# A hybrid RWKV-7 / latent-attention layer on one core: recurrence matmuls by head instead of by chunk parity, hi matmuls ahead of lo matmuls

## Chip, cores and metric

One core of a Trainium2 chip. The metric is device time in microseconds (us) of one execution of the kernel; lower is better.

## What is computed

One decoder layer, then a final norm, for 256 tokens of width 2048, all in float32. The parts that matter here:

```python
proj = rms_norm(x, attn_norm_g) @ w_in            # 35 column tiles of 128
# RWKV-7 group: 16 heads of 64; r, k, v, decay, a by token, then for each token t
state = state * w_t[:, None, :] + sa[..., None] * b_t[:, None, :] + v_t[..., None] * k_t[:, None, :]
y_t   = einsum('hvk,hk->hv', state, r_t)          # sa = state applied to a_t
y_rwkv = (group_norm(y) + bonus) * gate
# latent attention group: 8 heads, causal softmax
y = concat(y_rwkv, y_mla);  x = x + y @ w_out
x = x + conv_glu_ffn(rms_norm(x))                 # gate and up 2048 -> 5632, down 5632 -> 2048
```

## The kernel before, in words

**Dense products.** Every weight comes as pieces of 128x1024 float32 (512 KB) through SyncE's queue (`piece`, L121). ScalarE casts a piece to `hi` (L129), VectorE makes `lo = raw - hi` (L130), three buffers each. `prod_b` (L153) multiplies a piece of eight 128x128 weight blocks with activations that are themselves split in hi and lo: for each block j a matmul of `hi` with 512 moving columns (both parts of the activations, L157) and one of `lo` with 256 (L159), into one PSUM tile. It serves the input projection (`in_tile`), the up projections of the attention (`up_b`) and gate and up of the feed-forward part. `prod_a` (L169, L176 to L178) has the activations as weights and 512 moving columns throughout; it serves `wuv`, `wout` and the down projection.

**The recurrence.** The 256 tokens are cut into four chunks `c` of 64, c = 2w + par. `decay` (L391) makes the decays of two head pairs from two small matmuls (`lw` on array rows 0 to 63, `la` on rows 64 to 127). `gram` (L495) makes per head a 128x128 matrix of products within a chunk (`pg`, L507, 64 array rows each), masks it into `G1` on VectorE (L510), and sends blocks of it to a DRAM table `dL` (L519). `solve` (L540) reads `dL` back as `Lp` and inverts 32x32 triangles on VectorE (L548 to L554); `pR` and `pT` (L596, L609) join them into 64x64 inverses `TT`. `chunk(c)` (L624) then runs for both halves `hf` (8 heads each): `px` = state part (L635, one matmul of 128 moving columns for a pair of heads) plus local part (L639, 64x64); VectorE scales it into `xs` (L643); `TT` product (L648); ScalarE copies it into `UV` (L650); `pS` (L655) feeds the state update on VectorE (L674, L675); `py` = state part (L661) plus local part (L665), copied out by ScalarE (L678). The two heads of a pair are computed one after the other; the rows and columns of the array that a matmul uses depend on the parity of the chunk:

```python
rs_ = slice(par * 64, par * 64 + 64)
PE.matmul(px[rs_, a_ * P:(a_ + 1) * P], AR[pp][:, g, c, 0, :], ST[hf][:, a_, :], start=True, stop=True)
PE.matmul(px[rs_, e * 64:(e + 1) * 64], G1[c][hf][rs_, e, 0:64], UV[c][rs_, p, h * 64:h * 64 + 64], ...)
```

Each of these float32 matmul calls is two instructions in the trace (eight calls show as x16). The state update `pS` is the one product in which calls to the two column halves of the array (`hs`) already alternate.

**Order.** The program is written stage by stage; a scheduler of the framework puts each engine's instructions in order, and interleaves dense products of later stages (`mm`, on TensorE) with the recurrence. Engines run their lists in that order. `group_norm(w)` (L680) follows chunks 1 and 3; its VectorE work is interleaved too.

## Time and profile before

| | |
|---|---|
| time of the runs | 1240.6 us median of 3 (1240.4 to 1244.41) |
| the profiled execution: its own time, its span | 1240.28 us, 1238.5 us |
| busy: TensorE, VectorE, ScalarE, GpSimd | 97%, 67%, 48%, 5% |
| weights read | 210.48 MB, mean 174 GB/s of DMA |
| mean granted TensorE clock | 0.985 |

The busy time of a matmul in the trace includes its latency and overlaps the next one, so the pace of TensorE is read from the distance of one start to the next, not from the mean duration. Up to 75 us the kernel loads x and makes the first projections; Gram matrices come at 110 to 176 us, `solve` up to 244 us, the chunks from 255 to 361 us, softmax and attention up to 440 us, and from 490 us the feed-forward part.

### The profile page before, as it was taken

The page shows a single profiled execution, that of the slowest core. Times are in us where ns is not written, and L with a number is a line of the kernel's source. Part 1 is how long each engine was busy: PE and PEld are TensorE (multiplying, and loading weights), DVE is VectorE, ACT ScalarE, POOL GpSimd, SP SyncE. Part 2 cuts the span into 40 slices and gives each one's busy share as a digit, 9 for nine tenths or more (in the row PEclk, how much of TensorE's full clock was granted, in tenths as well). Part 3 has the DMA queues.
Part 4 walks back from the last instruction along what each step waited for, and adds up shares of the span by engine and source line. Part 5 has one row for each costly group of instructions (what it writes and reads, how often), then busy time and mean ns, then how long its engine had stood idle before and what let it go on. Part 6 is the DMA issues. An engine that isn't in the chain of part 4 may idle for free.

```text
span 1238.5 us, 18227 instructions
## 1 busy us (share of the span) xinstructions
PE 1206.4 (97%) x6897; PEld 1014.8 (82%) x6897; DVE 833.1 (67%) x1339; ACT 600.1 (48%) x931; POOL 56.6 (5%) x196
## 2 busy tenths in 40 slices
PE   6999979999999999999999999999999999999996
PEld 5778868888866788888888888888888888888885
DVE  6898749857766556777777776445567777775563
ACT  6784326534334445555555555333455555554452
POOL 4300000011011000100000000000000000000000
PEclk9999989999997999999999999999999999999999
DMA  8645444733423455555555555565655555566662
GB/s 298 212 133 158 132 124 140 217 120 112 133 69 102 153 171 181 167 194 190 187 188 187 187 188 187 187 202 190 199 190 187 187 188 187 187 220 211 213 204 88
DMA packets 70760, 215.80 MB, mean 174 GB/s; under 512 B 17360, under 2 KB 17616, under 8 KB 70672
## 3 DMA queue, kind: packets, MB, share of 16 engines
q1 hardware_dynamic: 69520, 211.84, 53.5%
q10 hardware_dynamic: 768, 2.05, 0.5%
q8 instruction: 54, 0.88, 0.3%
q0 software_dynamic: 384, 0.75, 0.2%
q14 instruction: 34, 0.28, 0.1%
HBM read 210.48 MB, written 3.41 MB: 173 GB/s over the span
## 4 chain that ended last, share of the span: by engine, by line
PE 93%; DVE 3%; DMA 2%; ACT 1%; issue 1%; POOL 1%; ACTq 0%; SPq 0%; DVEq 0%
PE mm L157 37%; PE mm L159 19%; PE mm L177 9%; PE mm L176 9%; PE mm L178 9%; PE pg L507 1%; PE px L639 1%; DVE lo L130 1%; PE px L648 1%; PE psc L819 1%; PE px L635 1%; PE py L665 1%; PE psc L817 1%; DMA raw<-in_win 1%; DMA cst<-in_cst 1%
## 5 line engine op out<-in xcount | busy, mean ns | idle before, releaser
L130 DVE TENSOR_TENSOR lo<-raw,hi 128x1024 fp32r<-128x1024 f32 x376 | 460.5, 1225 | 300.5 <-ACT hi L129 296.9
L129 ACT CAST hi<-raw 128x1024 fp32r<-128x1024 f32 x376 | 394.8, 1051 | 482.9 <-PE mm L157 232.0
L157 PE MATMUL mm<-z,hi 128*128 128x512 f32 x1408 | 493.5, 393 | 0.3 <-ACT hi L129 0.3
L159 PE MATMUL mm<-z,lo 128*128 128x256 f32 x1408 | 393.1, 279 | 0.8 <-DVE lo L130 0.8
L157 PEld LDWEIGHTS mm<-z,hi 128*128 128x128 f32 x1408 | 263.8, 187 | 63.4 <-ACT hi L129 0.6
L159 PEld LDWEIGHTS mm<-z,lo 128*128 128x128 f32 x1408 | 263.8, 187 | 1.2 <-DVE lo L130 1.1
L157 PE MATMUL mm<-x,hi 128*128 128x512 f32 x528 | 195.7, 408 | 16.7 <-DVE h L165 8.5
L159 PE MATMUL mm<-x,lo 128*128 128x256 f32 x528 | 153.8, 291 | 2.2 <-DVE lo L130 2.2
L157 PEld LDWEIGHTS mm<-x,hi 128*128 128x128 f32 x528 | 102.3, 194 | 41.0 <-ACT hi L129 8.2
L177 PE MATMUL mm<-lo,hh 128*128 128x512 f32 x336 | 130.7, 389 | 0.0
L178 PE MATMUL mm<-hi,hl 128*128 128x512 f32 x336 | 130.7, 389 | 0.0
L176 PE MATMUL mm<-hi,hh 128*128 128x512 f32 x336 | 119.4, 389 | 0.0
L159 PEld LDWEIGHTS mm<-x,lo 128*128 128x128 f32 x528 | 102.3, 194 | 5.4 <-DVE lo L130 2.7
L176 PEld LDWEIGHTS mm<-hi,hh 128*128 128x128 f32 x336 | 63.1, 188 | 13.2
L177 PEld LDWEIGHTS mm<-lo,hh 128*128 128x128 f32 x336 | 63.1, 188 | 13.1
L178 PEld LDWEIGHTS mm<-hi,hl 128*128 128x128 f32 x336 | 63.1, 188 | 13.0
L177 PE MATMUL mm<-lo,yhi 128*128 128x512 f32 x128 | 52.0, 406 | 0.1
L178 PE MATMUL mm<-hi,ylo 128*128 128x512 f32 x128 | 51.2, 400 | 0.0
L176 PE MATMUL mm<-hi,yhi 128*128 128x512 f32 x128 | 49.8, 403 | 0.0
L925 POOL MEMSET gt<- 128x2 f32 x44 | 4.4, 100 | 586.1 <-DVE hl L937 583.5
L177 PEld LDWEIGHTS mm<-lo,yhi 128*128 128x128 f32 x128 | 24.5, 192 | 6.2 <-DVE lo L130 0.5
L157 PE MATMUL mm<-cl,hi 128*128 128x512 f32 x80 | 29.6, 408 | 0.0
(284 smaller groups left out, 1189.7 us busy)
## 6 DMA issues: line engine op xcount, KB each, us to landing
raw<-in_wgu SPq DMA_DIRECT2D x176, 512.0 KB, 4.4
raw<-in_wdn SPq DMA_DIRECT2D x88, 512.0 KB, 4.3
raw<-in_win SPq DMA_DIRECT2D x70, 512.0 KB, 3.7
raw<-in_wout SPq DMA_DIRECT2D x32, 512.0 KB, 3.9
raw<-in_wuq SPq DMA_DIRECT2D x6, 512.0 KB, 3.8
xraw<-in_xT SPq DMA_DIRECT2D x4, 512.0 KB, 6.2
xt<-in_x SPq DMA_DIRECT2D x4, 512.0 KB, 6.7
raw<-in_wuk SPq DMA_DIRECT2D x4, 512.0 KB, 3.7
```

The lines of the kernel that those rows point to most:

```text
L129: S.copy(hi, raw)
L130: last_lo[0] = V.tensor_tensor(lo, raw, hi.bitcast(F32), ALU.subtract).ins
L157: PE.matmul(acc, hi[:, j * P:(j + 1) * P], ac, start=first and j == 0, stop=False, skip_group_check=True)
L159: PE.matmul(acc[:, :T], lo[:, j * P:(j + 1) * P], ac[:, 0, :], start=False, stop=last and j == n - 1, skip_group_check=True)
L176: PE.matmul(accs[tb], ah, wh, start=first and j == 0, stop=False)
L177: PE.matmul(accs[tb], ah, wl, start=False, stop=False)
L178: PE.matmul(accs[tb], al, wh, start=False, stop=last and j == n - 1)
L507: PE.matmul(pg[:, o:o + P], BK[pp][hs, gg, w, par * 2:par * 2 + 2, :], AR[pp][hs, gg, w * 2 + par, :, :], start=True, stop=True)
L635: PE.matmul(px[rs_, a_ * P:(a_ + 1) * P], AR[pp][:, g, c, 0, :], ST[hf][:, a_, :], start=True, stop=True)
L639: PE.matmul(px[rs_, e * 64:(e + 1) * 64], G1[c][hf][rs_, e, 0:64], UV[c][rs_, p, h * 64:h * 64 + 64], start=c == 0, stop=True, skip_group_ ...
L648: PE.matmul(pu[ru_, e * 64:(e + 1) * 64], TT[rs_, w * 16 + hf * 8 + e, :], xs[rs_, e * 64:(e + 1) * 64], start=True, stop=True, skip_group ...
L665: PE.matmul(py[rs_, e * 64:(e + 1) * 64], G1[c][hf][:, e, 64:128], UV[c][:, p, h * 64:h * 64 + 64], start=c == 0, stop=True, skip_group_ch ...
```

## The change

The rows of the recurrence are ordered by head of the pair: the first head of a pair always has output partitions 0 to 63 (array columns 0 to 63), the second 64 to 127, and calls of the two alternate (`pairs`). All contract over 128 rows: `XB`, a zeroed tile with the two heads' blocks on its diagonal, takes the place of `xs`; the lower half of `UV` starts at zero; the state part is two calls of 64 moving columns instead of one of 128. The chunk parity no longer picks rows. `xs` (one VectorE instruction per half) becomes two of `XB`, the copies to `UV` and `yt` become two each (one of the `UV` copies on VectorE), `dL` is written by 32 DMAs instead of 16, `pR` alternates its two column tiles, `gram` and `decay` issue the matmuls of the two row halves in turn, and `prod_b` issues the eight `hi` matmuls of a piece before its eight `lo` matmuls. Cut to its core:

```diff
--- before
+++ after
@@ prod_b
         hi, lo = pieces
         for j in range(n):
-            ac = act(kt0 + j)
-            PE.matmul(acc, hi[:, j * P:(j + 1) * P], ac, start=first and j == 0, stop=False,
+            PE.matmul(acc, hi[:, j * P:(j + 1) * P], act(kt0 + j), start=first and j == 0, stop=False,
                       skip_group_check=True)
-            PE.matmul(acc[:, :T], lo[:, j * P:(j + 1) * P], ac[:, 0, :], start=False,
+        for j in range(n):
+            PE.matmul(acc[:, :T], lo[:, j * P:(j + 1) * P], act(kt0 + j)[:, 0, :], start=False,
                       stop=last and j == n - 1, skip_group_check=True)
@@ decay
+        pw, pa = ch("lw"), ch("la")
         for g in range(2):
             p = pp * 2 + g
             cs = slice(g * T, (g + 1) * T)
-            pw, pa = ch("lw"), ch("la")
-            PE.matmul(pw[:, 0:T], lora[0:64, p * P:(p + 1) * P], wa[0:64], start=True, stop=True)
-            PE.matmul(pa[:, 0:T], lora[64:128, p * P:(p + 1) * P], wa[64:128], start=True, stop=True)
...
+            for rows, dst in ((slice(0, 64), pw), (slice(64, 128), pa)):
+                PE.matmul(dst[:, cs], lora[rows, p * P:(p + 1) * P], wa[rows], start=g == 0, stop=True,
+                          skip_group_check=True)
...
@@ gram
             for w in range(2):
+                pg = [ch("pg") for _ in range(2)]
+                for r in range(2):
+                    for gg in range(2):
+                        o = (r * 2 + gg) * P
+                        for h in range(2):
+                            hs = slice(h * 64, h * 64 + 64)
+                            PE.matmul(pg[h][:, o:o + P], BK[pp][hs, gg, w * 2 + r, :, :],
+                                      AR[pp][hs, gg, w * 2 + r, :, :], start=o == 0, stop=True,
+                                      skip_group_check=True)
                 for h in range(2):
-                    hs = slice(h * 64, h * 64 + 64)
-                    pg = ch("pg")
-                    for par in range(2):
-                        for gg in range(2):
-                            o = (par * 2 + gg) * P
-                            PE.matmul(pg[:, o:o + P], BK[pp][hs, gg, w, par * 2:par * 2 + 2, :],
-                                      AR[pp][hs, gg, w * 2 + par, :, :], start=True, stop=True)
...
                     for b in range(2):
-                        r0 = (1 - par) * 64 + b * 32
-                        k0 = par * 64 + b * 32 + w * 16 + hf * 8
-                        nc.sync.dma_start(dL[k0:k0 + 8].rearrange("e i t -> i e t"),
-                                          G1[c][hf][r0:r0 + 32, :, b * 32:(b + 1) * 32])
+                        r0 = 64 + b * 32
+                        for h in range(2):
+                            nc.sync.dma_start(dLv[b, c, :, h, hf * 4:hf * 4 + 4, :],
+                                              G1[c][hf][r0:r0 + 32, h * 4:h * 4 + 4, b * 32:(b + 1) * 32])
@@ UV
+    for c in range(4):
+        nc.gpsimd.memset(UV[c][64:128], 0.0)
...
-                S.copy(UV[w * 2 + par][rs_, pp * 2:pp * 2 + 2, :], ptv[rs_, :, w, :])
+                S.copy(UV[w * 2 + r][0:64, pp * 2:pp * 2 + 2, :], ptv[r * 64:r * 64 + 64, :, w, :])
@@ pR
-        for par in range(2):
-            r0, o0 = (1 - par) * 64, par * 64 + 32
-            for q in range(16):
-                qq = qh * 16 + q
-                PE.matmul(pr_[o0:o0 + 32, q * 32:(q + 1) * 32], G1[qh * 2 + par][q // 8][r0:r0 + 32, q % 8, 32:64],
-                          T11[0][r0:r0 + 32, qq, :], start=True, stop=True, tile_position=(r0, o0))
+        for q in range(16):
+            qq = qh * 16 + q
+            for h in range(2):
+                o0 = h * 64 + 32
+                PE.matmul(pr_[o0:o0 + 32, q * 32:(q + 1) * 32], G1[qq // 8][qq % 8 // 4][64:96, h * 4 + qq % 4, 32:64],
+                          T11[h][64:96, qq, :], start=True, stop=True, tile_position=(64, o0))
@@ chunk
+            def pairs(dst, terms):
+                for n, term in enumerate(terms):
+                    for a_ in range(4):
+                        p = hf * 4 + a_
+                        for h in range(2):
+                            lhsT, rhs = term(p, a_, h)
+                            PE.matmul(dst[HS[h], a_ * 64:(a_ + 1) * 64], lhsT, rhs,
+                                      start=n == 0 and a_ == 0, stop=True, skip_group_check=True)
+
+            def state(s):
+                return lambda p, a_, h: (AR[p // 2][:, p % 2, c, s, :], ST[hf][:, a_, HS[h]])
+
+            def local(s):
+                return lambda p, a_, h: (G1[c][hf][:, h * 4 + a_, s * 64:s * 64 + 64], UV[c][:, p, HS[h]])
+
+            pairs(px, ([state(0)] if c > 0 else []) + [local(0)])
+            for h in range(2):
+                V.tensor_tensor(XB[hf][HS[h], :, HS[h]], px[HS[h], 0:256].rearrange("p (a v) -> p a v", a=4),
+                                mtok[HS[h], c * 8 + hf * 4:c * 8 + hf * 4 + 4].unsqueeze(2).broadcast_to([64, 4, 64]),
+                                ALU.mult)
+            pu = px[:, 256:512]
+            pairs(pu, [lambda p, a_, h: (TT[:, c * 8 + p, :], XB[hf][:, a_, HS[h]])])
+            for h in range(2):
+                (S.copy if h else V.tensor_copy)(UV[c][64:128, hf * 4:hf * 4 + 4, HS[h]],
+                                                 pu[HS[h]].rearrange("p (a v) -> p a v", a=4))
             if c < 3:
                 pS = ch("pS")
...
+                pairs(pS, [lambda p, a_, h: (BKt[c][:, p, HS[h]], UV[c][:, p, HS[h]])])
+            pairs(py, ([state(1)] if c > 0 else []) + [local(1)])
...
-            ylast[c] = S.copy(yt[w][rs_, hf * 512:(hf + 1) * 512], py[rs_]).ins
+            for h in range(2):
+                yv = yt[w][rs_, hf * 512:(hf + 1) * 512].rearrange("p (a h v) -> p a h v", a=4, h=2)
+                ylast[c] = S.copy(yv[:, :, h, :], py[HS[h], 0:256].rearrange("p (a v) -> p a v", a=4)).ins
```

TensorE in the feed-forward part, two blocks of a `prod_b` piece before (names: `z` activations, `hi` and `lo` the two weight parts):

```order
L157 MATMUL mm_5050<-z_3981,hi_5053 128x512
L159 MATMUL mm_5050<-z_3981,lo_5054 128x256
L157 MATMUL mm_5050<-z_3981,hi_5053 128x512
L159 MATMUL mm_5050<-z_3981,lo_5054 128x256
```

and a whole piece now:

```order
L156 MATMUL mm_5394<-z_4067,hi_5419 128x512 x4
L156 MATMUL mm_5394<-z_4068,hi_5419 128x512 x4
L159 MATMUL mm_5394<-z_4067,lo_5420 128x256 x4
L159 MATMUL mm_5394<-z_4068,lo_5420 128x256 x4
```

The 512-column and 256-column matmuls of a piece stand in two runs instead of in turn.

TensorE at `px` of chunk 1, first half, before (L635 state part, L639 local part):

```order
L635 MATMUL px_2470<-ST_2384,AR_488 64x128
L639 MATMUL px_2470<-UV_1643,G_1180 64x64 x2
L635 MATMUL px_2470<-ST_2384,AR_488 64x128
L639 MATMUL px_2470<-UV_1643,G_1180 64x64 x2
L635 MATMUL px_2470<-ST_2384,AR_489 64x128
L639 MATMUL px_2470<-UV_1643,G_1180 64x64 x2
L635 MATMUL px_2470<-ST_2384,AR_489 64x128
L639 MATMUL px_2470<-UV_1643,G_1180 64x64 x2
```

and now:

```order
L658 MATMUL px_2495<-ST_2401,AR_488 64x64 x4
L658 MATMUL px_2495<-ST_2401,AR_489 64x64 x4
L658 MATMUL px_2495<-UV_1646,G_1175 64x64 x8
```

The state part has eight calls instead of four and no longer takes turns with the local part; both have the full 128 rows of weights.

SyncE's queue at the end of the Gram stage, before:

```order
L519 DMA dL<-G_1506 32x8x32 x2
L519 DMA dL<-G_1507 32x8x32 x2
L123 DMA raw_2065<-in_win 128x1024
L519 DMA dL<-G_1508 32x8x32 x2
L519 DMA dL<-G_1509 32x8x32 x2
L544 DMA Lp_1720<-dL 128x1024
L123 DMA raw_2087<-in_win 128x1024
```

and now:

```order
L527 DMA dL<-G_1509 32x4x32 x4
L527 DMA dL<-G_1510 32x4x32 x4
L527 DMA dL<-G_1511 32x4x32 x2
L527 DMA dL<-G_1512 32x4x32
L527 DMA dL<-G_1511 32x4x32 x2
L527 DMA dL<-G_1512 32x4x32 x3
L123 DMA raw_2051<-in_win 128x1024
L123 DMA raw_2082<-in_win 128x1024
L556 DMA Lp_1736<-dL 128x1024
L123 DMA raw_2104<-in_win 128x1024
```

In place of eight `dL` writes (of `G` tiles of the second half of the heads) there are sixteen, and the read of `Lp` stands behind two weight pieces.

VectorE in chunk 3 now (L669 `XB`, L675 the `UV` copy, L713 and L708 to L710 work of `group_norm(0)`):

```order
L669 TENSOR_TENSOR XB_2405<-px_2739,mtok 64x4x64 x2
L713 TENSOR_TENSOR gsq_3666<-UV_1645,bon 64x1024
L713 TENSOR_TENSOR gsq_3666<-UV_1646,bon 64x1024
L675 COPY UV_1648<-px_2739 64x4x64
L669 TENSOR_TENSOR XB_2406<-px_2787,mtok 64x4x64 x2
L708 TENSOR_TENSOR yt_2399<-yt_2399,ry_3671 128x1024
L709 TENSOR_TENSOR yt_2399<-yt_2399,gnw_3650 128x1024
L675 COPY UV_1648<-px_2787 64x4x64
L710 TENSOR_TENSOR yt_2399<-yt_2399,gnb_3651 128x1024
```

Two instructions of `group_norm(0)` of 1024 elements stand ahead of each of the two `UV` copies.

## Rows read from the trace of the kernel before

**Rows 1.** The page, parts 1 and 4: engines' busy time, and the chain by engine.

```profile
PE 1206.4 (97%) x6897; PEld 1014.8 (82%) x6897; DVE 833.1 (67%) x1339; ACT 600.1 (48%) x931; POOL 56.6 (5%) x196
...
PE 93%; DVE 3%; DMA 2%; ACT 1%; issue 1%; POOL 1%; ACTq 0%; SPq 0%; DVEq 0%
```

**Rows 2.** The windows view, three stretches; columns: stretch, then busy of each engine, clock, DMA.

```profile
184.00:244.00 60.00, 59.87 (x337) 52.20 (x337) 54.47 (x119) 35.63 (x62) 0.50 (x5) 0.96 0.57 166
...
259.10:361.10 102.00, 102.00 (x861) 82.43 (x860) 70.74 (x119) 38.13 (x64) 12.56 (x32) 0.99 0.38 121
361.10:394.00 32.90, 30.99 (x101) 19.23 (x100) 21.95 (x38) 13.20 (x29) 7.13 (x14) 0.79 0.15 49
```

**Rows 3.** Timeline of TensorE, second half of chunk 1; columns: start, busy, group (merged).

```profile
290.95 0.69 PE L655 MATMUL pS<-UV,BKt 128*64 128x64 f32 x16
291.47 0.39 PE L661 MATMUL py<-ST,AR 128*64 128x128 f32 x2
...
293.28 0.38 PE L635 MATMUL px<-ST,AR 128*64 128x128 f32 x2
...
296.17 0.50 PE L157 MATMUL mm<-cl,hi 128*128 128x512 f32 x1
```

**Rows 4.** The same view, the `TT` product of another half, and what follows it.

```profile
300.61 1.14 PE L648 MATMUL px<-xs,TT 64*64 64x64 f32 x16
301.68 0.49 PE L219 MATMUL rsb<-dg,ones 128*128 128x128 f32 x2
```

**Rows 5.** Chain of waits, long pieces: Gram, `pR`, and the local part of chunk 0.

```profile
123.65 1.64 PE pg L507 x16
...
244.37 3.86 PE pR L596 x128
...
255.19 1.07 PE px L639 x16
```

**Rows 6.** Timeline of TensorE in the feed-forward part: `prod_b` pairs and their weight loads.

```profile
659.79 0.39 PE L157 MATMUL mm<-z,hi 128*128 128x512 f32 x1
...
660.02 0.28 PE L159 MATMUL mm<-z,lo 128*128 128x256 f32 x1
660.02 0.19 PEld L157 LDWEIGHTS mm<-z,hi 128*128 128x128 f32 x1
660.14 0.39 PE L157 MATMUL mm<-z,hi 128*128 128x512 f32 x1
```

**Rows 7.** The same view in the down projection: 512-column matmuls only (`prod_a`).

```profile
799.63 0.39 PE L178 MATMUL mm<-hi,hl 128*128 128x512 f32 x1
...
800.76 0.39 PE L177 MATMUL mm<-lo,hh 128*128 128x512 f32 x1
```

**Rows 8.** Groups of VectorE, 244 to 362 us: tile, count | busy, mean ns | idle before.

```profile
L643 DVE TENSOR_TENSOR xs<-px,mtok 64x512 f32<-64x512 f32 x8 | 5.5, 689 | 7.6 <-PE px L639 7.6
L674 DVE TENSOR_TENSOR ST<-pS,ST 64x256 f32<-64x256 f32 x8 | 3.4, 420 | 0.9 <-PE py L661 0.7
...
L698 DVE TENSOR_TENSOR gsq<-UV,bon 64x1024 f32<-64x1024 f32 x2 | 2.4, 1215 | 0.0
```

**Rows 9.** Groups of the whole run: `prod_b`'s two largest, and a `decay` matmul.

```profile
L157 PE MATMUL mm<-z,hi 128*128 128x512 f32 x1408 | 493.5, 393 | 0.3 <-ACT hi L129 0.3
...
L157 PE MATMUL mm<-x,hi 128*128 128x512 f32 x528 | 195.7, 408 | 16.7 <-DVE h L165 8.5 <-ACT hi L129 8.2
...
L396 PE MATMUL lw<-sh,lora 64*128 64x256 f32 x16 | 5.6, 428 | 0.0
```

**Rows 10.** Timeline of SyncE's queue around the `dL` round trip.

```profile
174.11 1.96 SPq L519 DMA_DIRECT2D dL<-G  x4
178.67 0.34 SPq L544 DMA_DIRECT2D Lp<-dL  x1
```

**Rows 11.** The waits view of TensorE, first 600 us: total, times, longest.

```profile
PE mm L157 <- DVE h L165: 8.5, 2, 8.0
PE mm L159 <- DVE lo L130: 3.0, 2, 2.2
```

More of the change, by code (lines that the diff above doesn't have):

```diff
@@ L474, in hybrid_layer @@
     dL = dr.tile([P, 32, 32], F32, name="dL")
+    dLv = dL.rearrange("(h b c p) i t -> b c i h p t", h=2, b=2, c=4)
     boP = ch("boP")
-    bon = con([P, 32], "bon")
+    bon = con([64, 64], "bon")
     for p in range(8):
@@ L495, in gram @@
             hf = p // 4
[L496 removed]
+            e0 = (pp % 2) * 2
             for c in range(4):
@@ L533, in hybrid_layer, with bonus_rows @@
             pend.append(gram)
-    pend.append(lambda: V.tensor_copy(bon, boP[:, 0:32]))
+    def bonus_rows():
+        for r in range(2):
+            V.tensor_copy(bon[:, r * 32:r * 32 + 32], boP[r * 64:r * 64 + 64, 0:32])
+    pend.append(bonus_rows)
     TT = con([P, 32, 64], "TT")
@@ L584, in hybrid_layer @@
         for w in range(2):
[L585 to L587 removed]
+            for r in range(2):
+                S.copy(UV[w * 2 + r][0:64, pp * 2:pp * 2 + 2, :], ptv[r * 64:r * 64 + 64, :, w, :])
     RT = sv("RT").rearrange("p (q s) -> p q s", q=32)
@@ L604, in hybrid_layer @@
         pr_ = ch("pT")
-        for par in range(2):
-            r0, o0 = par * 64 + 32, par * 64
+        for h in range(2):
+            r0, o0 = h * 64 + 32, h * 64
             for q in range(16):
@@ L610, in hybrid_layer @@
                           TT[r0:r0 + 32, qq, 32:64], start=True, stop=True, tile_position=(r0, o0))
-        for par in range(2):
-            o0 = par * 64
+        for h in range(2):
+            o0 = h * 64
             V.tensor_copy(TT[o0:o0 + 32, qh * 16:(qh + 1) * 16, 32:64],
@@ L620, in hybrid_layer @@
         nc.gpsimd.memset(ST[hf], 0.0)
+    XB = [sb.tile([P, 512], F32, tag="xs", name=nm("XB"), bufs=2).rearrange("p (a t) -> p a t", a=4) for _ in range(2)]
+    for hf in range(2):
+        nc.gpsimd.memset(XB[hf], 0.0)
+    HS = (slice(0, 64), slice(64, 128))
     ylast = [None] * 4
     def chunk(c):
-        w, par = c // 2, c % 2
-        rs_ = slice(par * 64, par * 64 + 64)
-        ru_ = slice((1 - par) * 64, (1 - par) * 64 + 64)
+        w, r = c // 2, c % 2
+        rs_ = HS[r]
         for hf in range(2):
@@ L630, in chunk @@
             py = ch("py")
-            for a_ in range(4):
-                p = hf * 4 + a_
-                pp, g = p // 2, p % 2
-                if c > 0:
-                    PE.matmul(px[rs_, a_ * P:(a_ + 1) * P], AR[pp][:, g, c, 0, :], ST[hf][:, a_, :],
-                              start=True, stop=True)
-                for h in range(2):
-                    e = a_ * 2 + h
-                    PE.matmul(px[rs_, e * 64:(e + 1) * 64], G1[c][hf][rs_, e, 0:64], UV[c][rs_, p, h * 64:h * 64 + 64],
-                              start=c == 0, stop=True, skip_group_check=True)
@@ L641, in chunk @@
-            xs = sb.tile([P, 512], F32, tag="xs", name=nm("xs"), bufs=2)
-            mq = mtok.rearrange("p (w a h) -> p w a h", w=2, h=2)
-            V.tensor_tensor(xs[rs_].rearrange("p (a h v) -> p a h v", a=4, h=2),
-                            px[rs_].rearrange("p (a h v) -> p a h v", a=4, h=2),
-                            mq[rs_, w, hf * 4:hf * 4 + 4, :].unsqueeze(3).broadcast_to([64, 4, 2, 64]), ALU.mult)
-            pu = px
-            for e in range(8):
-                PE.matmul(pu[ru_, e * 64:(e + 1) * 64], TT[rs_, w * 16 + hf * 8 + e, :], xs[rs_, e * 64:(e + 1) * 64],
-                          start=True, stop=True, skip_group_check=True)
@@ L651, in chunk @@
+            pu = px[:, 256:512]
+            pairs(pu, [lambda p, a_, h: (TT[:, c * 8 + p, :], XB[hf][:, a_, HS[h]])])
+            for h in range(2):
+                (S.copy if h else V.tensor_copy)(UV[c][64:128, hf * 4:hf * 4 + 4, HS[h]],
+                                                 pu[HS[h]].rearrange("p (a v) -> p a v", a=4))
             if c < 3:
                 pS = ch("pS")
-                for e in range(8):
-                    hs = slice((e % 2) * 64, (e % 2) * 64 + 64)
-                    PE.matmul(pS[hs, (e // 2) * 64:(e // 2 + 1) * 64], BKt[c][:, hf * 4 + e // 2, hs],
-                              UV[c][:, hf * 4 + e // 2, hs], start=True, stop=True)
@@ L657, in chunk @@
-            for a_ in range(4):
-                p = hf * 4 + a_
-                pp, g = p // 2, p % 2
-                if c > 0:
-                    PE.matmul(py[rs_, a_ * P:(a_ + 1) * P], AR[pp][:, g, c, 1, :], ST[hf][:, a_, :],
-                              start=True, stop=True)
-                for h in range(2):
-                    e = a_ * 2 + h
-                    PE.matmul(py[rs_, e * 64:(e + 1) * 64], G1[c][hf][:, e, 64:128], UV[c][:, p, h * 64:h * 64 + 64],
-                              start=c == 0, stop=True, skip_group_check=True)
+                pairs(pS, [lambda p, a_, h: (BKt[c][:, p, HS[h]], UV[c][:, p, HS[h]])])
```

79 lines of the change are left out of this document (38 added, 41 removed).

## The prediction

> **What bounds the kernel now.** I read the page first: TensorE is busy 97% of the span, VectorE 67%, and the chain that ended last lies on TensorE for 93% [rows 1]. So a TensorE instruction that takes less pace shortens the kernel, as long as nothing else takes over. Then the windows view by stage: in the chunk stage (259 to 361 us) TensorE is busy throughout, at a granted clock of 0.99; VectorE is busy 70.7 of 102 us, ScalarE 38.1 [rows 2]. The recurrence's own waits are filled there by dense products, so what the recurrence saves on TensorE lets that filling end earlier. The waits view names the exceptions: TensorE waits 8.0 us once for VectorE's `h` (before 184 us, behind the round trip of `dL`), and 3.0 us in two waits for `lo` [rows 11]. Last comes the timeline, for the pace of each product, taken from start to start, since a matmul's own duration overlaps the next one.
>
> **The chunks.** Where calls to the two column halves alternate today (`pS`), 16 instructions take 291.47 − 290.95 = 0.52 us. Those that use one half take: `py` 293.28 − 291.47 = 1.81, `px` 296.17 − 293.28 = 2.89 [rows 3], `TT` 301.68 − 300.61 = 1.07 [rows 4]. After the change all are `pS`'s kind: 128 rows, 64 columns of the array, 64 moving columns, halves in turn. `px` and `py` become 32 instructions each, so 1.04, and `TT` 0.52. A half with state goes from 0.52 + 1.81 + 2.89 + 1.07 = 6.29 to 3.12 and saves 3.17; six such halves save 19.0. In chunk 0 `px` and `TT` take 1.07 each [rows 4, 5] and `py` some 0.9 (estimated as half of `py` with state), all going to 0.52: 1.5 per half, 3.0 for two. On TensorE that is **22.0 us**, the upper end.
>
> VectorE limits how much of it arrives. Per half it loses `xs` (0.69) and gains two `XB` and one `UV` copy of 64x256, 0.42 each by the `ST` update of that shape [rows 8]: 3 × 0.42 − 0.69 = +0.57, for eight halves +4.6, so 75.3 us in this stage. The busiest VectorE beside an unbroken TensorE is 54.47 of 60 us, 91% [rows 2]. At 91% the 75.3 us need 82.7, a saving of 19.3. I go below this because in chunk 3 two instructions of `group_norm(0)`, 1.2 us each [rows 8], stand ahead of each `UV` copy in VectorE's order, and `pS` or `py` and, through them, the dense products listed behind, wait for it. I take **−17**. The lower end is 10: 12 us lost, a wait of 1.5 us in each of eight halves, somewhat over one such instruction.
>
> **`pR`.** 128 instructions take 3.86 us, 30 ns each [rows 5], already near the 32 ns of an alternating `pS` instruction [rows 3], though with half the moving columns. Alternating may halve it (−1.9) or give nothing; **−1**.
>
> **Gram.** Sixteen instructions of one row half take 1.64 us, 102 ns each [rows 5], eight groups in all. No row shows alternating row halves with 128 moving columns; by `pS`, with twice its columns, an instruction would take 65 ns, 0.6 us less a group [rows 3, 5]. In the order of the changed kernel three groups alternate fully and two in part, the others still run half by half. Between 0 and −2.4, **−1.5**.
>
> **`decay`.** The 32 small matmuls (16 `lw` of 0.43 us each with latency [rows 9], as many `la`) stay, and only one group of four newly alternates; halving that group's would give 32 × 0.43 / 4 / 2 = 1.7 at most, much of it latency: **0**, at most 1 either way.
>
> **`hi` ahead of `lo`.** A pair takes 660.14 − 659.79 = 0.35 us, `hi` to `lo` 0.23 and `lo` to `hi` 0.12 [rows 6]. In the down projection 512-column matmuls follow each other at (800.76 − 799.63) / 5 = 0.226 [rows 7]. A piece of eight blocks takes 2.80 now. Reordered it is seven `hi` to `hi` (7 × 0.226), one `hi` to `lo`, one `lo` to `hi`, and seven `lo` to `lo` of unknown pace L: 1.93 + 7 L. If the switch costs nothing, L = 0.35 − 0.226 = 0.124 and nothing is gained; if L is the 0.12 (unrounded 0.1175) of a `lo` followed by a `hi`, a piece takes 2.76 and gains 0.042. There are 1408 + 528 pairs in the two largest groups [rows 9] and 112 in three small ones, 2048 in all, or 256 pieces: the gain is 0 to 10.7; I take the middle, **−5.6**. A `lo` is also first needed 1.6 us later in its piece, which may remove the 3.0 us of waits for it [rows 11]: **−1**.
>
> **The `dL` round trip.** Four `dL` writes occupy SyncE for 1.96 us [rows 10]. There are 16 more, eight of them in the last half of the heads: 8 × 0.49 = 3.9 us, but most leave while Gram runs. The read of `Lp`, which took SyncE at 178.67, now stands behind two weight pieces. Its landing ends the wait for `h` of 8.0 us [rows 11], because VectorE's `solve` work stands ahead of `h`. Better: the extra writes are half the size and land earlier (−1). Worse: the queue delays it by 3. **+1**.
>
> **Nothing:** the zeroing on GpSimd (5% busy [rows 1]); `bon`, the key norms and the second `T11` (a few small instructions ahead of stages where TensorE has other products); `yt`, two smaller ScalarE copies instead of one, with ScalarE at 38 of 102 us [rows 2]; were that cover gone, `py`'s buffer would hold up the next chunk.
>
> **Clock.** After a thin stretch the granted clock is low: 0.79 from 361 to 394 us, where TensorE has gaps and short matmuls [rows 2]. Shorter chunks end with the same thin stretch: 0, ±3.
>
> **Sum.** −17 − 1 − 1.5 − 5.6 − 1 + 1 = −25.1. Against the profiled execution's own 1240.28 (0.3 below the median of 1240.6) that is **1215 us**.
>
> **The rivals.**
>
> *VectorE becomes the bound of the chunk stage.* For it: 70.7 us plus 4.6 in a stage that is to take 85 is 89%, and its list has long instructions ahead of the `UV` copies [rows 2, 8]. Against: 91% with TensorE unbroken has been seen [rows 2]. With 8 us of the 22 left the sum is −16: **1224**; with 0 left, 1232. The Trainium skill, "TensorEngine Tiling (Array Packing)", section "PSUM Bottleneck", warns of this: tiling speeds up TensorE and not the work that empties PSUM, which may become the bottleneck. The trace before agrees as far as the two engines' loads go; no run yet shows the evacuation late.
>
> *The change of order of `hi` and `lo` gives nothing*, since the 0.12 and 0.23 may just be how the 0.35 is split between two records [rows 6]. Then L = 0.124: **1221**.
>
> *Slower: a run of `lo` matmuls is paced by its weight loads.* A 256-column matmul lasts shorter than its load, whose record takes 0.19 [rows 6]. Today every second matmul is a long one that covers it. If in a run of eight each load had to end before its matmul starts, L would be 0.19 and 1792 steps (256 × 7) would cost 1792 × (0.19 − 0.12) = 125 us: **1340**. It decides the sign once L is over 0.12 + 25 / 1792 = 0.134. Against: the load of a `hi` starts at 660.02, with a `lo` matmul, and its own matmul starts 0.12 later, before the load's record ends [rows 6]; the next `lo` should do the same. The Trainium skill, "TensorE: Matmul & The Clock Gate", section "The mechanism", says that a weight load overlaps a running matmul only when the two use different row groups; by that every full-array `lo` run would pay. The 0.12 of these rows, and the unbroken 0.226 of 512-column matmuls, both full-array, speak against it.
>
> *The stall at 184 us grows.* If `Lp` comes 8 us later (once more the wait there is) and the clock is at its lower level for ten more microseconds behind it, 8 + 10 / 2 = 13 us are lost instead of 1: **1227**. Together with a bound VectorE and no gain from the order that is 1237 to 1243, the case in which nothing shows.
>
> **How the numbers follow.** My forecast, 1203 to 1222 by its own ends: 0.60. VectorE the bound, 1220 to 1232: 0.21. No gain from the order, 1217 to 1225: 0.09. The stall alone, 1224 to 1231: 0.03. Nothing left, 1237 to 1243: 0.03. Slower by loads: 0.04. The low end: −22 − 1.9 − 2.4 − 10.7 − 3 = −40 gives 1200, which needs all ends at once; I take **1203**. The high end takes in most of VectorE's case: **1230**. A measurement of this kernel can tell 0.3%, 3.7 us, from no change: faster 0.91 (all but nothing left and the loads), within 0.04, slower 0.05, with a little of the nothing-left case on that side.
>
> **What the profile after would show.** Right: `px`, `TT` and `py` at 0.52 us per 16 instructions; the chunk stage some 17 us shorter with TensorE still without gaps; a piece of `prod_b` at about 2.77 us with L at 0.12. Wrong: TensorE gaps in the chunk stage released by VectorE's `UV` copy or `XB`; products that keep their 1.07 us per 16 although halves alternate; L above 0.124; or a wait around 184 us well over 8 us.

## The result, and the profile after

| | before | after |
|---|---|---|
| median of the runs | 1240.5 us (4 runs, 1235.55 to 1244.41) | 1224.34 us (4 runs, 1222.87 to 1226.5) |
| the profiled execution: its own time, its span | 1240.28, 1238.5 | 1224.32, 1222.5 |

The ratio is 0.9873, with a 95% interval of 0.9835 to 0.9912: 16 us less, where 25 were forecast and the range went from 1203 to 1230. On another chip the same kernel had 1226.4 against 1240.6, a ratio of 0.9892 (0.9865 to 0.9918).

One execution of a variant (`hi` and `lo` in turn for gate and up alone) took 6570 us at a mean granted clock of 0.16 and is left out of that variant's ratio; it counts in the median of 1223.51 us given below, and the other five have a median of 1223.3.

The page of the changed kernel, parts 1 and 4, says what it said before [rows 1]: TensorE bounds it, and its share of the chain is 90%.

```profile
PE 1186.5 (97%) x6993; PEld 1001.6 (82%) x6993; DVE 837.9 (69%) x1359; ACT 599.7 (49%) x939; POOL 60.4 (5%) x202
```

To see where the time went I cut the span at five points that both traces have: the end of the wait behind the `dL` round trip, the last `py`, and the first and last gate or up matmul of the feed-forward part. The windows view gives a row for each stretch; its columns are the stretch, the length, the busy time of TensorE, weight loads, VectorE, ScalarE and GpSimd, the granted clock, the DMA share and GB/s. Before:

```profile
0.00:184.10 184.10, 164.49 (x957) 138.00 (x957) 136.16 (x294) 101.62 (x176) 24.45 (x73) 0.97 0.58 178
...
184.10:361.20 177.10, 177.06 (x1499) 148.63 (x1499) 133.72 (x252) 76.12 (x129) 16.88 (x51) 0.98 0.45 138
361.20:493.40 132.20, 130.29 (x559) 98.96 (x560) 80.70 (x121) 60.98 (x112) 7.13 (x14) 0.95 0.43 140
493.40:1119.70 626.30, 625.22 (x3405) 539.24 (x3404) 420.63 (x593) 313.46 (x454) 8.19 (x58) 1.00 0.58 190
```

And after:

```profile
0.00:184.20 184.20, 163.88 (x958) 138.72 (x958) 136.89 (x299) 102.60 (x176) 29.32 (x79) 0.97 0.57 178
...
184.20:343.00 158.80, 155.89 (x1595) 133.08 (x1595) 136.18 (x267) 75.31 (x136) 15.40 (x51) 0.97 0.51 154
343.00:474.10 131.10, 128.02 (x559) 97.11 (x560) 82.10 (x123) 61.11 (x113) 6.76 (x14) 0.97 0.43 141
474.10:1103.40 629.30, 629.30 (x3405) 542.75 (x3404) 421.12 (x594) 312.63 (x454) 8.96 (x58) 1.00 0.58 189
```

Up to the wait's end nothing changed (184.1 and 184.2 us). `solve`, `pR`, `pT` and the chunks went from 177.1 to 158.8 us, **18.3 less**. The attention part went from 132.2 to 131.1. The up projections, whose only change is the order of `hi` and `lo`, went from 626.3 to 629.3 us, **3.0 more**: 1.1 us of waits in it are gone (1119.70 − 493.40 = 626.30, of which TensorE is busy for 625.22), and the matmuls themselves take 4.1 us longer. These make −16.3 with the 0.1 at the start, against −15.96 between the two executions; the last stretch took 0.3 more.

In the timeline of TensorE of the changed kernel (columns: start, duration, group merged) a half of chunk 1 reads so, to be set against [rows 3, 4]:

```profile
290.25 0.27 PE L658 MATMUL pS<-UV,BKt 128*64 128x64 f32 x1
...
291.23 0.69 PE L658 MATMUL py<-UV,G 128*64 128x64 f32 x16
291.70 0.69 PE L658 MATMUL px<-ST,AR 128*64 128x64 f32 x16
292.17 0.68 PE L658 MATMUL px<-UV,G 128*64 128x64 f32 x16
292.78 1.20 PE L156 MATMUL mm<-cl,hi 128*128 128x512 f32 x4
...
297.81 0.69 PE L658 MATMUL px<-XB,TT 128*64 128x64 f32 x16
298.43 1.20 PE L156 MATMUL mm<-cl,hi 128*128 128x512 f32 x4
```

`pS` and `py` together, 48 instructions, take 291.70 − 290.25 = 1.45 us (2.33 before); `px`, 32 instructions, 292.78 − 291.70 = 1.08 (2.89 before); `TT` 298.43 − 297.81 = 0.62 with the hand-over to the next product (1.07 before). Summed from start to start over the whole run, without waits, the chunk products went from 43.9 to 23.7 us, 20.2 less. `pR` went from 3.86 to 2.42, Gram from 15.9 to 13.2.

The pieces of the feed-forward part, to be set against [rows 6]:

```profile
656.27 2.03 PE L156 MATMUL mm<-z,hi 128*128 128x512 f32 x8
658.14 1.12 PE L159 MATMUL mm<-z,lo 128*128 128x256 f32 x8
659.10 2.03 PE L156 MATMUL mm<-z,hi 128*128 128x512 f32 x8
```

A piece takes 659.10 − 656.27 = 2.83 us; eight `hi` take 1.86 (0.233 each) and eight `lo` 0.96 (0.120 each). Before, a piece was eight pairs of 0.350 to 0.351.

The waits view of TensorE, whole run (total, times, longest), to be set against [rows 11]:

```profile
PE mm L156 <- DVE h L165: 7.5, 2, 7.2
PE ssP L447 <- ACT ksq L443: 3.1, 1, 3.1
...
PE py L658 <- DVE UV L675: 1.3, 1, 1.3
PE mm L156 <- DVE cr L165: 1.1, 1, 1.1
...
PE mm L159 <- DVE lo L130: 0.7, 1, 0.7
PE mm L156 <- DVE kn L165: 0.4, 1, 0.4
```

The wait for `h` behind `dL` is 7.2 instead of 8.0 us and the waits for `lo` fell from 3.0 to 0.7 (1.5 us of that near 11 us, 0.8 in the feed-forward part). The wait for `ksq` near 68 us grew from 0.6 to 3.1 us, the waits in the softmax from 1.5 to 2.9, and 2.8 us in the chunk stage (`UV`, `cr`, `kn`) are new; it had no wait at all before.

### The profile page after: what moved, and what is told of

Same layout as the page of the kernel before. It is cut to its first block, busy times and chain, and to the rows that moved or that the text cites. A ratio compares the mean times of both kernels' runs of the same rounds, so it can differ in the third digit from the quotient of the medians.

```text
span 1222.5 us, 18434 instructions
## 1 busy us (share of the span) xinstructions
PE 1186.5 (97%) x6993; PEld 1001.6 (82%) x6993; DVE 837.9 (69%) x1359; ACT 599.7 (49%) x939; POOL 60.4 (5%) x202
## 4 chain that ended last, share of the span: by engine, by line
PE 90%; DVE 3%; DMA 2%; ACT 2%; issue 1%; POOL 1%; SPq 0%; ACTq 0%; DVEq 0%; POOLq 0%
PE mm L156 38%; PE mm L159 19%; PE mm L177 9%; PE mm L178 9%; PE mm L176 9%; PE pg L514 1%; DMA raw<-in_win 1%; DVE lo L130 1%; ACT hi L129 1%; PE px L658 1%; DMA rp<-in_pos 0%; DMA Lp<-dL 0%; PE psc L834 0%; PE py L658 0%; PE psc L832 0%
## 5 line engine op out<-in xcount | busy, mean ns | idle before, releaser
L130 DVE TENSOR_TENSOR lo<-raw,hi 128x1024 fp32r<-128x1024 f32 x376 | 460.5, 1225 | 294.1 <-ACT hi L129 288.1
L156 PE MATMUL mm<-z,hi 128*128 128x512 f32 x1408 | 356.9, 395 | 0.0
L156 PEld LDWEIGHTS mm<-z,hi 128*128 128x128 f32 x1408 | 253.3, 188 | 48.8
L159 PEld LDWEIGHTS mm<-z,lo 128*128 128x128 f32 x1408 | 192.8, 188 | 15.4
L159 PE MATMUL mm<-z,lo 128*128 128x256 f32 x1408 | 197.7, 282 | 0.0
L156 PE MATMUL mm<-x,hi 128*128 128x512 f32 x528 | 147.2, 415 | 15.7 <-DVE rp L249 8.2
L178 PE MATMUL mm<-hi,hl 128*128 128x512 f32 x336 | 130.7, 389 | 0.0
L156 PEld LDWEIGHTS mm<-x,hi 128*128 128x128 f32 x528 | 98.7, 198 | 35.6 <-ACT hi L129 8.2
L176 PE MATMUL mm<-hi,hh 128*128 128x512 f32 x336 | 119.7, 389 | 0.0
L159 PEld LDWEIGHTS mm<-x,lo 128*128 128x128 f32 x528 | 75.3, 192 | 8.8 <-DVE lo L130 1.5
L159 PE MATMUL mm<-x,lo 128*128 128x256 f32 x528 | 81.3, 290 | 0.7 <-DVE lo L130 0.7
L176 PEld LDWEIGHTS mm<-hi,hh 128*128 128x128 f32 x336 | 63.1, 188 | 13.1
L178 PEld LDWEIGHTS mm<-hi,hl 128*128 128x128 f32 x336 | 63.1, 188 | 13.0
L178 PE MATMUL mm<-hi,ylo 128*128 128x512 f32 x128 | 50.6, 396 | 0.0
L176 PE MATMUL mm<-hi,yhi 128*128 128x512 f32 x128 | 49.1, 398 | 0.0
L176 PEld LDWEIGHTS mm<-hi,yhi 128*128 128x128 f32 x128 | 24.2, 189 | 5.2
```

Source lines behind the costliest of these rows:

```text
L130: last_lo[0] = V.tensor_tensor(lo, raw, hi.bitcast(F32), ALU.subtract).ins
L156: PE.matmul(acc, hi[:, j * P:(j + 1) * P], act(kt0 + j), start=first and j == 0, stop=False, skip_group_check=True)
L159: PE.matmul(acc[:, :T], lo[:, j * P:(j + 1) * P], act(kt0 + j)[:, 0, :], start=False, stop=last and j == n - 1, skip_group_check=True)
L176: PE.matmul(accs[tb], ah, wh, start=first and j == 0, stop=False)
L178: PE.matmul(accs[tb], al, wh, start=False, stop=last and j == n - 1)
```

## Experiments

Each ratio is to runs of the kernel before on the same chip, whose median there was 1240.6 to 1242.4 us. The changed kernel itself has 0.9873 on one chip and 0.9892 on another, each with some 0.003 or 0.004 to either side, so by its time alone a variant between 0.985 and 0.991 is not told from it; what follows rests on the pieces of the traces. Each trace is one execution.

### `hi` and `lo` in turn again in the changed kernel

```diff
-        for j in range(n):
-            PE.matmul(acc, hi[...], act(kt0 + j), ...)
-        for j in range(n):
-            PE.matmul(acc[:, :T], lo[...], act(kt0 + j)[:, 0, :], ...)
+        for j in range(n):
+            PE.matmul(acc, hi[...], act(kt0 + j), ...)
+            PE.matmul(acc[:, :T], lo[...], act(kt0 + j)[:, 0, :], ...)
```

> The changed kernel with the hi and lo matmuls of a piece in turn again, as before; all else stays. Theory (the new order costs about 21 ns a piece: 2833 ns mean in the trace after against 2811 before, 256 pieces, 5.5 us, less 1.5 to 2.3 us of waits for lo that it removed): about 1220 us, pieces at 2.81 us, and TensorE waits for lo of some 3 us back. Rival A (the order as such is neutral, the slower pace came from other work on the chip): 1224 us with pieces still at 2.83. Rival B (my forecast, the order gains): 1230 us.

Measured: 1224.78 us (ratio 0.9867, 0.9839 to 0.9896), no difference that can be told from the changed kernel. The windows show why the time alone would mislead:

```profile
182.50:347.50 165.00, 159.80 (x1594) 135.60 (x1594) 137.80 (x268) 74.93 (x136) 16.53 (x51) 0.94 0.49 149
...
479.30:1105.60 626.30, 625.21 (x3404) 538.75 (x3404) 420.69 (x593) 313.43 (x454) 7.88 (x58) 1.00 0.58 190
...
247.00:265.00 18.00, 18.00 (x306) 16.25 (x300) 10.52 (x19) 3.54 (x5) 4.70 (x14) 0.72 0.37 134
```

The up projections are back at 626.3 us, with pieces of 2.81 us on average: the price of the order, 4.1 us there less 1.1 us of waits, is as the theory has it. But the stretch with the chunks takes 165.0 instead of 158.8. Its granted clock is 0.94 (0.97 in the changed kernel) and most of that lies between 247 and 265 us, in and behind `pR` and `pT`: 0.72 there. In the changed kernel the same 18 us read:

```profile
247.00:265.00 18.00, 18.00 (x338) 16.09 (x337) 13.06 (x23) 4.21 (x6) 2.78 (x14) 0.91 0.38 134
```

TensorE is busy for all of them in both. By the clock's records 10.2 us of those 18 are at the lower level (half of the other) in the one and 3.4 in the other, so some 3 of the 6 us are the clock's; another 2.3 us are waits in the chunk stage (5.1 against 2.8, by the waits view). The clock's part can't be put down to the order of the matmuls: the variant with `hi` and `lo` in turn for gate and up alone (below) has the changed kernel's matmuls in the same order up to 478 us, and its trace shows

```profile
247.00:265.00 18.00, 18.00 (x311) 16.24 (x310) 11.55 (x21) 3.41 (x6) 2.81 (x14) 0.72 0.34 118
```

So in the up projections the order costs what its pace says, and rival A is wrong about the pace. That the time does not show it is due to a lower clock in this execution, which is not shown to come with the edit, and to the waits.

### The new order alone, in the kernel before

The edit is `prod_b`'s part of the change and nothing else.

> The kernel before with only the new order in prod_b. Theory: pieces at 2.83 us, slower by 3.5 to 5.5 us, so 1244 to 1246. Rival A (neutral): 1240.5. Rival B (the forecast's term and the lo waits): 1234.

Measured: 1248.92 us, ratio 1.0061 (1.004 to 1.0082): **slower**, by 7.3 us. The trace has the same 629.3 us for the up projections, and again a lower clock in the stretch with the recurrence:

```profile
182.80:365.40 182.60, 182.60 (x1499) 153.83 (x1500) 134.42 (x252) 76.31 (x130) 16.60 (x51) 0.95 0.43 134
...
497.30:1126.60 629.30, 629.30 (x3405) 542.76 (x3404) 421.34 (x594) 312.75 (x454) 8.95 (x58) 1.00 0.59 189
```

The waits for `lo` fell to 0.9 us, as forecast, and the wait for `dL` ended 1.3 us earlier. Taken alone this part of the change loses in this trace 3.0 us in the up projections, and 5.5 in the stretch with the recurrence (182.6 against 177.1). There 19.6 us are at the lower clock level, 7.8 in the kernel before; half of the difference is 5.9 us and covers the 5.5. Whether that lower clock comes with the order or with the execution is not shown.

### The chunks without alternation

The same instructions, all first heads of a product and then all second heads:

```diff
-                    for a_ in range(4):
-                        p = hf * 4 + a_
-                        for h in range(2):
+                    for h in range(2):
+                        for a_ in range(4):
+                            p = hf * 4 + a_
```

> The changed kernel with each product of the chunks done for all first heads, then for all second heads: the same instructions, no alternation of column halves. Theory (alternation is what halves the pace): the chunk products go from some 31 to 34 ns an instruction to 58, that is 672 x 0.025 = 17 us more on TensorE, 1238 to 1242 us. Rival (128 rows of weights and one column half per head are what helped, the order of calls does not matter): 1224 us, products at 0.52 us per 16 instructions still.

Measured: 1228.75 us, ratio 0.9904 (0.9874 to 0.9934): 4 us more than the change (2.4 more than on the other chip), not 17, and by the ratios not clear of noise. The chunk products took 31.4 us in all instead of 23.7, an increase of 7.7. The trace tells why it is less than half of the theory's:

```profile
295.34 0.22 PE L658 MATMUL pS<-UV,BKt 128*64 128x64 f32 x1
295.40 0.22 PE L658 MATMUL py<-ST,AR 128*64 128x64 f32 x1
295.40 0.22 PE L658 MATMUL pS<-UV,BKt 128*64 128x64 f32 x1
295.46 0.22 PE L658 MATMUL py<-ST,AR 128*64 128x64 f32 x1
```

The scheduler lays the second heads of `pS` beside the first heads of `py`, so two column halves still run in turn; here a `py` and a `pS` start together at 295.40, and the next `py` 0.06 later. Where one column half really follows itself the pace is 58 ns an instruction (the median of such starts in the trace), where halves alternate a pair takes 58. So the mechanism is shown by the pace, instruction by instruction, and the experiment's own expectation was wrong about how much alternation the edit removes.

### `decay` as before

> The changed kernel with decay as before (per pair its own lw and la tile, the tanh of a pair right behind its two matmuls). Theory (the 3.1 us wait for ksq near 68 us comes from the tanh and the copies now bunched ahead of it on ScalarE): that wait goes back to under 1 us, 1221 to 1222.5 us. Rival (the wait comes with the order that the new prod_b gives the scheduler, decay is innocent): the wait stays at about 3 us, 1224 us.

Measured: 1229.86 us, ratio 0.9909 (0.9883 to 0.9935). The 3.1 us wait for `ksq` is gone (1.0 us for `tw` stands in its place), so that wait does belong to the new `decay`. But the kernel is no faster, and its profiled execution is 2.9 us longer; the gain went into the next wait:

```profile
185.71 0.80 PE L156 MATMUL mm<-x,hi 128*128 128x512 f32 x1 [9.78 <-DVE h L165]
```

TensorE arrives 1.0 us earlier and waits 9.8 us for the `dL` round trip instead of 7.2. That wait ended 1.5 us later, since the last Gram group, with which the round trip begins, ended 1.6 us later (174.2 instead of 172.6): 942 matmuls stand ahead of its last one, 928 in the changed kernel.

### `gram` and `pR` half by half

```diff
-                for r in range(2):
-                    for gg in range(2):
-                        o = (r * 2 + gg) * P
-                        for h in range(2):
+                for h in range(2):
+                    for r in range(2):
+                        for gg in range(2):
+                            o = (r * 2 + gg) * P
...
-        for q in range(16):
-            for h in range(2):
+        for h in range(2):
+            for q in range(16):
```

> The changed kernel with gram's and pR's matmuls in the order of one half after the other. Theory (row halves in turn save on gram what column halves save on the chunks): gram's matmuls go from 13.2 to 15.9 us and pR's from 2.4 to 3.9, so 1228.5 us. Rival (the gain on these is taken back by the wait around 184 us, which starts when the last Gram matrices are written): that wait shrinks by as much, 1224 us.

Measured: 1229.63 us, ratio 0.9905 (0.9879 to 0.9932). Gram took 15.6 instead of 13.2 us and `pR` 4.5 instead of 2.4. Yet the wait for `dL` ended earlier, and was 3.1 us shorter, Gram having grown by 2.4:

```profile
182.02 3.68 PE L156 MATMUL mm<-x,hi 128*128 128x512 f32 x8 [4.12 <-DVE h L165]
```

So for Gram the rival is right in this trace. The scheduler laid 48 matmuls behind the last Gram call, where the changed kernel has 28; so the round trip began earlier, and more work stood under it. The profiled execution is 5.9 us longer than that of the change all the same, and this came later: 20.5 us are at the lower clock between the wait and the last `py` (8.3 in the changed kernel), which is some 6 us, and the wait for `UV` is 2.4 us instead of 1.3. `pR`'s 2.1 us lie in the same stretch, part of them by that clock, and are not separated.

### The new rows and columns alone

`prod_b`, `decay`, the order of `gram` and of `pR` as before; the chunk's change and its layouts stay.

> The change of rows and column halves alone: prod_b, decay, the order of gram and of pR as before. Theory (the chunks give some 20 us on TensorE and 3 us of new waits there; pR 1.4, gram 0.9 to 2.7 and the order of prod_b together give little): 1224 to 1228 us with the chunk products at 24 us in all. Rival (the other parts carry several us of the gain): 1232 us.

Measured: 1223.53 us, ratio 0.9852 (0.9824 to 0.988). The chunk products take 23.6 us, and the whole gain of the change is there with one of its parts.

### `hi` and `lo` in turn for gate and up alone

> The changed kernel with hi and lo in turn again for gate and up of the feed-forward part alone (all but its first two pieces); everything up to 480 us keeps its order. Theory (174 pieces at 2.81 us instead of 2.83, and the earlier stages left alone): the stretch of the up projections goes from 629.3 to 626.3 us, 1221 us in all. Rival (the first experiment of this kind gained nothing because the order of eight is worth something in the feed-forward part too): 1224 us, with new TensorE waits after 480 us.

Measured: 1223.51 us, ratio 0.9846 (0.982 to 0.9872). Its up projections took 624.7 us:

```profile
478.20:1102.90 624.70, 624.70 (x3405) 539.24 (x3404) 420.03 (x593) 314.00 (x454) 8.12 (x58) 1.00 0.58 190
```

That is 4.6 us less than in the changed kernel, by the pace, and 1.6 less than in the kernel before, which waits 1.1 us for `hi` and `lo` at the start of the stage; the two pieces of the new order avoid that. The time shows only part of that: between the last `py` and the up projections 13.7 us are at the lower clock (9.1 in the changed kernel), and 15.9 between the wait for `dL` and the last `py` (8.3), although TensorE's matmuls come in the changed kernel's order up to 478 us.

### Both `UV` copies on ScalarE

```diff
-                (S.copy if h else V.tensor_copy)(UV[c][64:128, ...], ...)
+                S.copy(UV[c][64:128, ...], ...)
```

> The changed kernel with both UV copies on ScalarE. Theory (VectorE, with group_norm's instructions ahead of its UV copy, makes the 3.1 us of TensorE waits in the chunk stage): the wait of py for UV (1.3 us) and most of the waits behind joined copies (1.4 us) go, 1222 us. Rival (those waits come from the length of the chain from px to pS itself; two copies one after the other on ScalarE make it longer): waits stay or grow, 1224 to 1226 us.

Measured: 1224.63 us, ratio 0.9865 (0.9839 to 0.989), no difference. The timeline of the changed kernel shows the copies' place in chunk 3:

```profile
339.72 1.23 DVE L709 TENSOR_TENSOR yt<-yt,gnw 128x1024 f32<-128x1024 f32 x1
340.98 0.42 DVE L675 COPY UV<-px 64x256 f32<-64x256 f32 x1
...
341.43 0.37 ACT L675 COPY UV<-px 64x256 f32<-64x256 f32 x1 [3.55 <-DVE UV L675]
...
341.45 1.52 PE L658 MATMUL py<-UV,G 128*64 128x64 f32 x16 [1.31 <-DVE UV L675]
```

VectorE's copy starts behind `yt` of `group_norm(0)` (1.23 us), and TensorE's `py` waits 1.31 us for it. ScalarE's copy begins 0.03 us after VectorE's has ended, after 3.55 us of idling, since it waits for the semaphore that VectorE's copy raises: an order that the program sets between two writes of one tile, and no limit of the engines that is shown. With both on ScalarE the wait moved one step up the chain, to `XB`, which stays on VectorE:

```profile
337.11 0.86 DVE L669 TENSOR_TENSOR XB<-px,mtok 64x256 f32<-64x256 f32 x2
...
338.02 0.69 PE L658 MATMUL px<-XB,TT 128*64 128x64 f32 x16 [1.42 <-DVE XB L669]
```

So VectorE's order is the cause, as the theory has it, and the copy was the wrong thing to move.

### `group_norm(0)` off VectorE, and the parts that lose undone

Two kernels: first `prod_b` and `decay` as before with the rest of the change, then the same with four long instructions of `group_norm(0)` on GpSimd.

```diff
+        G_ = nc.gpsimd if w == 0 else V
-        V.tensor_tensor(y, y, gnwb[0], ALU.mult)
-        V.tensor_tensor(y, y, gnwb[1], ALU.add)
+        G_.tensor_tensor(y, y, gnwb[0], ALU.mult)
+        G_.tensor_tensor(y, y, gnwb[1], ALU.add)
...
-            V.tensor_tensor(sq[HS[r]]..., UV[w * 2 + r]..., bq..., ALU.mult)
+            G_.tensor_tensor(sq[HS[r]]..., UV[w * 2 + r]..., bq..., ALU.mult)
```

> The changed kernel with prod_b and decay as before; chunks, gram and pR as in the change. Theory (each part adds up in TensorE time: chunks alone 1223.5 us in the run before, gram 2.7 and pR 1.4 less): 1219 to 1220 us. Rival (what gram and pR save before 184 us is handed to the wait there and to the waits in the chunk stage): 1223 to 1225 us.

> The same, and four of group_norm(0)'s long VectorE instructions (the bonus product twice, the weight and the bias) on GpSimd. Theory (these stand ahead of the UV copies and XB of chunk 3 in VectorE's order and make its waits): the TensorE wait for UV near 340 us goes from 2.4 us to under 0.5, 2 us less than the kernel without this edit. Rival (the wait is only moved to the next VectorE instruction, or GpSimd makes group_norm late for the projection behind): no difference, or 1 to 3 us more.

> The changed kernel itself on the same chip, as the measure for the two others: 1224.3 us, within 3.

Measured, all on one chip with the kernel before at 1240.61 us: the change itself 1226.4 (1224.89 to 1229.26), with `prod_b` and `decay` as before 1221.18 (1220.3 to 1222.22; ratio 0.9844, 0.9816 to 0.9872), with `group_norm(0)` moved too **1215.71** (1214.93 to 1217.06; ratio 0.9801, 0.9773 to 0.9828). The three sets of times do not overlap. The last one beats both kernels. Its waits, as the waits view has them:

```profile
PE mm L157 <- DVE h L165: 11.3, 3, 10.7
...
PE pyT L723 <- DVE yt L719: 3.8, 1, 3.8
...
PE px L654 <- DVE XB L665: 0.9, 1, 0.9
...
PE px L654 <- DVE ST L685: 0.5, 1, 0.5
```

The wait for `UV`, 2.5 us in the kernel next to it, is gone, and so is one of 1.6 us in the softmax; one of 3.8 us for `group_norm(0)`'s result is new. The time fell by 5.5 us, more than the 2 expected; the profiled spans differ by 5.2. Between the wait for `dL` and the last `py` they differ by 2.2 us (158.6 against 160.8), as the removed wait would have it; 1.5 us lie ahead of it, and 1.2 us in the attention part, where 3.4 us fewer are at the lower clock. Ahead of the wait, too, 3.0 us fewer are at the lower level, so the clock alone would make 1.5 and 1.7 us there. The four executions of the last kernel have mean clocks of 0.987 to 0.990, those of the kernel next to it 0.983 to 0.986. So 2.2 us fit the edit, and whether the rest is its work is open. The first of these kernels came out between its theory (1219 to 1220) and its rival (1223 to 1225): its last Gram group ended 2.3 us earlier than in the changed kernel (170.3 against 172.6), but its wait for `dL`, now 10.7 us, only 0.8 us earlier (183.4 against 184.2).

## Why the prediction was right or wrong

The direction was right, the time was inside the range, and the size was off by 9 us. The mechanism of the chunks, which carries the gain, was right; the terms for the order of `hi` and `lo` and for the stage ahead of 184 us were not. Point by point:

- **The chunks, −17, and `pR`, −1.** Measured −18.3 for the whole stretch from 184 us to the last `py`, 18 forecast. On TensorE alone the chunks gave 20.2 of the 22.0 counted, and the waits that VectorE's order makes took 2.8 back. The rival with VectorE as the bound named the right place (the `UV` copy behind `group_norm(0)`) at too high a price: 1.3 us behind a `UV` copy and 1.4 behind copies of dense products, in place of a wait in every half. `XB` took 422 ns and the copy 418, as priced by [rows 8]. `pR` measured −1.4.
- **`hi` ahead of `lo`, −5.6.** This step failed. I wrote a piece as seven `hi` to `hi` at 0.226, the pace of the down projection [rows 7], plus 7 L. L came out at 0.120, where I had put it; but `hi` to `hi` takes 0.233, no less than `hi` to `lo` does [rows 6], and the step from the last `lo` to the next `hi` 0.125 instead of 0.118. A piece takes 2.83 instead of 2.81 us. In the up projections alone (176 of the 256 pieces) the pace is +4.1 in place of −3.9, and +3.0 with the waits that went. Both ends that I gave (0 and −10.7) rested on a pace taken from another stage, so the true value lay outside them.
- **Gram −1.5, the waits for `lo` −1, the round trip +1, and the share of `prod_b` ahead of 184 us.** Gram saved 2.7 us and the waits for `lo` 1.5 ahead of 184 us, both more than forecast, and yet the wait behind the `dL` round trip ended at 184.1 before and at 184.2 after. Two things took them. Up to the last Gram group, which ended at 172.8 before and at 172.6 after, other waits grew by 2.9 us (`ksq`, `tw`), and 6.8 us instead of 3.4 are at the lower clock level. Behind it the round trip runs: VectorE's mask, the `dL` writes, the read of `Lp`, `solve`. The chain view has its two ends, before and after:

```profile
171.70 1.08 PE pg L507 x8
...
178.67 3.31 DMA Lp<-dL
...
171.50 1.09 PE pg L514 x8
...
176.47 5.56 DMA Lp<-dL
```

The writes were done earlier, so the read began 2.2 us earlier, but it took 5.56 us instead of 3.31 to land. The term of the round trip had both (writes earlier, read delayed behind weight pieces); from the last Gram group to the wait's end it came to 11.6 us instead of 11.3. Over all thirteen traces the read took 3.3 us with no weight piece issued in the 2 us before it, 4.5 to 5.2 with one (five traces), and 5.5 to 5.9 with two (seven). In the ten kernels of the experiments with other edits the wait ended between 181.9 and 185.7, with 4.1 to 10.7 us of idling in front; TensorE came to it between 171.2 and 177.9 us, and its end did not follow that. I had read that wait off [rows 11] as a cost of its own and added the terms ahead of it as if it were not there.
- **`decay`, 0.** It did bring a wait of 3.1 us for `ksq` (that its four `tanh`, bunched on ScalarE, are the reason is likely and not shown). What this costs in the end is open: without it the last Gram group came later, not earlier.
- **Clock, 0 ± 3.** In the changed kernel it was neutral (0.985 and 0.986 over the run). In its variants it was worth as much as the terms under study, which is why the experiments are read by stretches. That the term was 0 is in part luck: six executions of the changed kernel on the second chip had mean clocks from 0.981 to 0.985 and took 1229.3 to 1224.9 us.
- **The rivals.** "The order gives nothing", 1221, was nearer than the forecast, and still too kind. The run of `lo` paced by its weight loads did not happen: L is 0.120, not the 0.19 of a load's record, so the loads do not pace the run. The Trainium skill's rule of "TensorE: Matmul & The Clock Gate", section "The mechanism", by which a load overlaps a running matmul only in other row groups, does not hold for these rows; the same section also has loads into a background weight buffer pulled ahead of running matmuls, and these rows would fit that. The stall at 184 us did not grow: it was 7.2 us instead of 8.0, because TensorE came to it 0.8 us later. `dL`'s eleven last writes took SyncE 5.5 us, but were issued from 169.8 us on, and the read of `Lp` took SyncE at 176.5, ahead of the 178.7 of [rows 10]:

```profile
169.77 5.50 SPq L527 DMA_DIRECT2D dL<-G  x11
...
176.47 0.33 SPq L556 DMA_DIRECT2D Lp<-dL  x1
```

- **Two sums.** The case in which nothing shows comes by its own terms to 1242 us with 8 us of the chunks left and to 1250 with none, not to 1237 to 1243; and the chances named for faster add up to 0.93, not 0.91. Neither touches the forecast.

## What to carry to other kernels

On a saturated TensorE, small products with 64 output columns should be ordered so that calls to the two column halves stand in turn: a pair then takes the time of one, which was worth 20 of 44 us here and needed only another layout of rows and heads. Before savings are summed, mark the waits at the end of a long chain (here from the last Gram matrices through DRAM and VectorE) and ask on which side of the chain's start a saving lies: what is saved in the work that runs beside the chain only lengthens the wait, and what is saved ahead of its start counts if the chain keeps its length, which here hung on the weight pieces issued just ahead of its read. A pace is taken from a row of the same stage; a neighbour of the same shape was 3% off, and over 256 pieces that turned the sign of a term. And before a clock is put down to an edit, look for a trace with the same order of matmuls.

## What the runs showed of the hardware that was not expected

- Matmuls of the same shape (128x512, f32) and clock level have two paces: 0.226 to 0.227 us in the down projection, and 0.233 in the up projections, whether `hi` follows `hi` or `lo` follows. Which operand moves is not the reason: `wout` has the weights moving on the same three lines as the down projection (L176 to L178) and a median of 0.232 to 0.233 at the higher clock level. What is the reason is open; no run here tried it.
- The granted clock differs between executions that issue the same matmuls in the same order: 0.91 and 0.72 in the 18 us from 247 to 265 in the changed kernel and in the one with gate and up in turn, whose matmuls are the same up to 478 us, with TensorE busy for all of them in both.
- The landing of a DMA read of 512 KB (`Lp`) took 3.3 us with no piece of 512 KB issued on the same queue in the 2 us before (one trace), 4.5 to 5.2 with one (five traces) and 5.5 to 5.9 with two (seven).
- While GpSimd ran the two bonus products, VectorE's state update in SBUF beside them took 1.74 and 1.24 us instead of 0.43, while `XB`, which reads PSUM, kept its 0.43. The timeline of the kernel with `group_norm(0)` on GpSimd:

```profile
329.04 3.94 POOL L710 TENSOR_TENSOR gsq<-UV,bon 64x1024 f32<-64x1024 f32 x2
...
329.48 1.74 DVE L685 TENSOR_TENSOR ST<-ST,PC 64x256 f32<-64x256 f32 x1
...
332.02 1.24 DVE L685 TENSOR_TENSOR ST<-ST,PC 64x256 f32<-64x256 f32 x1
```

The first of these updates ended at 331.22, just behind the first product (329.04 and half of 3.94), the second at 333.26, just behind the other's end at 332.98: they read as held until GpSimd was done. The Trainium skill, "Trainium Architecture — The Big Picture", section "What this means for kernel authors", says that VectorE and GpSimd share a port pair under an exclusive lock; these rows agree. It still paid: TensorE waited 0.5 us for such an update, where it had waited 2.5 for `UV`.
